# Retention pairs: a sum kept in the dead half of the raw weights, a decay table behind the values, and early output products behind the last head's values product

## The chip, the cores and the metric

The kernel runs on one core of a Trainium2 chip. Time is device time of that core in microseconds (us). A kernel is timed in several runs; one further execution is taken by the hardware profiler, and its trace is what the rows below come from. Engines are named as the profile names them: PE is the matrix engine (PEld its weight loads), DVE, ACT and POOL are the vector, scalar and GpSimd engines, SP is the engine that issues most of the loads. Line numbers such as L1198 are lines of the kernel before.

## The reference

The kernel computes a trunk of four layers on 512 tokens of 1024 channels: layer 0 and layer 3 mix tokens with a convolution module, layer 1 with neighbourhood attention, layer 2 with retention; a gated convolutional feed-forward follows each. All in float32. The change lies in the retention layer:

```python
def retention_mixer(h, w_in, log2_inv_decay, gn_g, w_out):
    q, k, v, g = jnp.split(h @ w_in, [hk, 2 * hk, 2 * hk + hv], axis=-1)
    q = rotary(q.reshape(b, s, RET_HEADS, RET_KEY_DIM)).transpose(0, 2, 1, 3)
    k = (rotary(k.reshape(b, s, RET_HEADS, RET_KEY_DIM)) * (RET_KEY_DIM ** -0.5)).transpose(0, 2, 1, 3)
    ...
    o = (o_fwd + o_bwd).transpose(0, 2, 1, 3)
    mu = jnp.mean(o, axis=-1, keepdims=True)
    var = jnp.mean(jnp.square(o - mu), axis=-1, keepdims=True)
    o = ((o - mu) * lax.rsqrt(var + EPS)).reshape(b, s, hv).astype(h.dtype) * gn_g
    return (jax.nn.silu(g) * o) @ w_out
```

`o_fwd` and `o_bwd` are sums over earlier and later tokens, weighted by a decay that falls with distance. There are 4 heads, with keys of 256 and values of 512 channels.

## The kernel before

**Precision.** A float32 operand is split into a high part (a cast on ACT, L208 for activations and L182 for weights) and a low part (a subtraction on DVE, L209 and L183). Each product is three matmuls: high by high, high by low, low by high (`mm3`, L198 to L200; for values `mm3s`, L203 to L205; the output projection has its own loop at L1420).

**Weights.** `load_w` brings a block of 128x1024 floats (512 KB) by a load that SP issues (L173) into a raw tile, tag `wr`. The pool of raw tiles has three of them (`NRAW = 3`), which all weights of the kernel take in turn: a load waits until the last reader of the tile three loads earlier is done. The halves go to pools of three as well.

**Retention.** The decay is applied as one table for each head (`table`, L1238 to L1247: a load, six instructions on DVE, an Exp on ACT; one buffer), so that a head's scores are a masked product, `scores` (L1327 multiplies by the table), and `av` multiplies scores by values, takes mean and variance of each of four banks (L1382, L1383) and normalises them (L1371). The function `gate` transposes the result (L1399), multiplies it by the gate (L1402) and splits it; `wout` multiplies by the output weights and adds into the residual in memory (`xd`); for the last two heads, `part` and `pair_wout` keep the sums of both in one bank.

**Sevens.** The projections for queries, keys and gates of heads 1 to 3 are made in pairs with seven block products in place of eight (`seven`, L1216). `sums` loads two combinations of weight blocks into a tile with tag `ws` (two of them, `RWS = 2`): a broadcast load from SP (L1172), then an accumulating load from POOL (L1175); and a fourth block d into one of two fixed tiles, `sqacc` and `dd` (L1177). `weights` (L1180 to L1201) loads a raw tile `r1`, splits it, adds its first half to the second half of the `ws` tile (L1190), splits that, adds d to that sum (L1194), and splits d and the new sum into one pair of tiles, `h4` and `l4`. The last two products of a seven need `h4` and `l4`; they are left pending and made inside the next seven or where `finish` is called; L1214 then adds the bank on DVE. Inside a seven, ACT copies sums from the bank (L1225, L1228) and writes a negated copy (L1232).

**Order.** The kernel is written once as a program; a scheduler of the language, which simulates the engines, orders each engine's instructions, with the written order as priority. `tc.issue_after(x)` holds what is written in it behind instruction x. Each engine then runs its own list in order. The loop over heads stands at L1453: table, scores, gate products, `av`, the next head's queries and keys, gate, values, output.

Of the kernel before, what the change touches and what calls it, by code (L numbers as in the profile page):

```python
# [14 lines left out]
MUL, ADD, SUB = ALU.mult, ALU.add, ALU.subtract  # L15
# [4 lines left out]
D = 1024  # L20
# [78 lines left out]
def tile_trunk(  # L99
# [7 lines left out]
    nc = tc.nc  # L107
# [9 lines left out]
    def nm(s):  # L117
        uid[0] += 1
        return f"{s}{uid[0]}"
# [9 lines left out]
    psa, psb = "a", "b"  # L129

    def bank(which):
        return cur[which].tile([P, T], F32, tag="ps", name=nm("ps"))
# [43 lines left out]
    def load_w(src, n, eng=nc.vector):  # L176
        return split_w(load_raw(src, n), n, eng)
# [19 lines left out]
    def mm3(o, wh, wl, ah, al, first, last, free=False):  # L197
        nc.tensor.matmul(o, wh, ah, start=first, stop=False, skip_group_check=free)  # L198
        nc.tensor.matmul(o, wh, al, start=False, stop=False, skip_group_check=free)  # L199
        nc.tensor.matmul(o, wl, ah, start=False, stop=last, skip_group_check=free)  # L200

    def mm3s(o, wh, wl, ah, al, first, last):
        nc.tensor.matmul(o, ah, wh, start=first, stop=False)  # L203
# [3 lines left out]
    def split(src, hi, lo, n=None):  # L207
        state["cast"] = nc.scalar.copy(hi, src)  # L208
        return nc.vector.tensor_tensor(lo, src, hi.bitcast(F32), SUB)  # L209
# [38 lines left out]
    state = {"late": [], "squares": []}  # L248
# [881 lines left out]
    def ret(after):  # L1130
        LR = 2
        with ExitStack() as st:
# [47 lines left out]
            def weights(src, r13, d):  # L1180
                n = T
                if MACC:
                    r1 = load_raw(src[:, :D], D)
                    w1 = acc_w(r1, src[:, :D], D)
                else:
                    r1 = load_raw(src[:, :D], D)
                    w1 = split_w(r1, D, nc.vector)
                w13 = split_w(r13, D, nc.vector)
                r2 = r13[:, n:]
                nc.vector.tensor_tensor(r2, r2, r1[:, :n], ADD)  # L1190
                h2 = rp.tile([P, T], F32R, tag="h2", name=nm("h2"))
                l2 = rp.tile([P, T], F32R, tag="l2", name=nm("l2"))
                split(r2, h2, l2)
                nc.vector.tensor_tensor(r13[:, :n], r2, d, ADD)  # L1194
                h4 = rp.tile([P, D], F32R, tag="h4", name=nm("h4"))
                l4 = rp.tile([P, D], F32R, tag="l4", name=nm("l4"))
                split(d, h4[:, n:], l4[:, n:])
                split(r13[:, :n], h4[:, :n], l4[:, :n])  # L1198
                u = lambda w, b: (w[0][:, b * n:(b + 1) * n], w[1][:, b * n:(b + 1) * n])
                return {"a11": u(w1, 0), "a22": u(w1, 1), "s3": u(w13, 0), "s1": u(w13, 1),  # L1200
                        "s2": u((h2, l2), 0), "sg": u((h4, l4), 0), "a12": u((h4, l4), 1)}  # L1201
# [36 lines left out]
            def table(h):  # L1238
                tb = rp.tile([P, DTAB], F32, tag="dt", name=nm("dt"))
                nc.scalar.dma_start(tb, rel)  # L1240
                for c in (slice(0, DTAB // 2), slice(DTAB // 2, DTAB)):
                    t2 = t512()[:, :DTAB // 2]
                    nc.vector.tensor_scalar(t2, tb[:, c], 0.0, lgam[:, 4 + h:5 + h], ALU.min, MUL)
                    nc.vector.tensor_scalar(tb[:, c], tb[:, c], 0.0, lgam[:, h:h + 1], ALU.max, MUL)
                    nc.vector.tensor_tensor(tb[:, c], tb[:, c], t2, SUB)
                nc.scalar.activation(tb, tb, AF.Exp)
                return tb  # L1247
# [36 lines left out]
            def vproj(h):  # L1284
                pss = [bank(psb if h == 0 else psa) for _ in range(4)]
                for kc in range(4):
                    if h in VACC:
                        wh, wl = load_w_acc(ret_v[h, kc], D)
                        for t in range(3):
                            for tb in range(4):  # L1290
                                for i in range(2):
                                    k = kc * 2 + i
                                    q = slice(tb * P, (tb + 1) * P)
                                    nc.tensor.matmul(
                                        pss[tb], (xhi, xlo)[t == 1][k][:, q],
                                        (wh, wl)[t == 2][:, i * T:(i + 1) * T],
                                        start=k == 0 and t == 0, stop=k == KD - 1 and t == 2)
                        continue
                    wh, wl = load_w(ret_v[h, kc], D)
                    for tb in range(4):  # L1300
                        for i in range(2):
                            k = kc * 2 + i
                            s = slice(i * T, (i + 1) * T)
                            q = slice(tb * P, (tb + 1) * P)
                            mm3s(pss[tb], wh[:, s], wl[:, s], xhi[k][:, q], xlo[k][:, q],
                                 k == 0, k == KD - 1)
                vv = []
                for tb in range(4):
                    hi = rp.tile([P, T], F32R, tag=f"v{tb}h", name=nm("vh"))
                    lo = rp.tile([P, T], F32R, tag=f"v{tb}l", name=nm("vl"))  # L1310
                    t = t512()
                    nc.scalar.activation(t, pss[tb], AF.Copy, scale=rstd_col[:, tb:tb + 1])
                    split(t, hi, lo)
                    vv.append((hi, lo))
                return vv
# [94 lines left out]
            def wout(h, yy, outs=range(4)):  # L1410
                for o2 in outs:
                    acc = h in WACC
                    w = load_w_acc(ret_out[h, o2], D) if acc else load_w(ret_out[h, o2], D)
                    pss = [bank(psa), bank(psa)]
                    for t in ((0, 1), (2,)) if acc else ((0, 1, 2),):
                        for oi in range(2):
                            for e in range(4):
                                s = slice((oi * 4 + e) * P, (oi * 4 + e + 1) * P)
                                for j in t:
                                    nc.tensor.matmul(pss[oi], w[j == 2][:, s], yy[e][j == 1],  # L1420
                                                     start=e == 0 and j == 0, stop=e == 3 and j == 2)
                    for oi in range(2):
                        r = t512()
                        nc.scalar.copy(r, pss[oi])
                        nc.gpsimd.dma_start(xd[o2 * 2 + oi], r, accum_op=ADD)
# [23 lines left out]
            vv = vproj(0)  # L1449
            for p in range(4):  # L1450
                combos(p)
            gs = None
            for h in range(RH):  # L1453
                tb = table(h)
                aa = scores(h, qk, tb)
                if h < 3:
                    gs, rest = g_seven(h) if h or G0 else gproj(h)
                else:
                    finish()
                    rest()  # L1460
                    wout(2, yy, (3,))
                oo = av(h, aa, vv)
                if h < 3:
                    qa, qb = seven("q", h + 1, 0), seven("q", h + 1, 1)
                    rest()
                    qk = rope(0, qa)
                    yy = gate(h, oo, gs, 0, 4)
                    finish()
                    qk += rope(1, qb)
                    vv = vproj(h + 1)  # L1470
                    if h < 2:
                        wout(h, yy)
                    else:
                        gs, rest = g_seven(3)
                else:
                    wout(2, yy, (2,))
                    for k in range(KD):
                        x[k] = const.tile([P, T], F32, tag=f"x{k}", name=nm("x"))
                        nc.gpsimd.dma_start(x[k], xd[k])
                    early = [[bank(psa), bank(psa)] for _ in range(2)]  # L1480
                    pair_wout(early[0], 2, 0, yy, True, False)
                    w = load_w(ret_out[2, 1], D)
                    part(early[1][0], w, yy, 0, True, False)
                    y3 = gate(h, oo, gs, 0, 4)
                    part(early[1][1], w, yy, 1, True, False)
                    for o2 in (0, 1):
                        pair_wout(early[o2], 3, o2, y3, False, True)
                    for o2 in (2, 3):
                        pair_wout([bank(psa), bank(psa)], 3, o2, y3, True, True)
# [215 lines left out]
```

## Time and profile before

| | us |
|---|---|
| median of 3 runs | 2529.01 |
| lowest and highest run | 2528.30, 2531.76 |
| the profiled execution | 2530.51 |
| its span | 2528.6 |
| PE busy in it | 2502.4 |
| DVE, ACT, POOL busy | 1862.7, 1319.8, 409.0 |

Mean granted clock of PE over the span is 0.997 of full speed. The retention layer lies between about 1180 and 1600 us of the span.

A row of the timeline is: start in us, duration in us, engine, line, operation, output<-inputs by the program's names, sizes, how many instructions the row joins (x3), and in brackets how long the engine stood idle before it and what ended that. A row of waits is: engine, what waited, what ended the wait, then total us, how many times, longest. The ends of matmuls are modelled, so the spacing of their starts is the better measure.

### The profile page before, as it was taken

The page shows a single profiled execution, that of the slowest core. Times are in us where ns is not written, and L with a number is a line of the kernel's source. Part 1 is how long each engine was busy: PE and PEld are TensorE (multiplying, and loading weights), DVE is VectorE, ACT ScalarE, POOL GpSimd, SP SyncE. Part 2 cuts the span into 40 slices and gives each one's busy share as a digit, 9 for nine tenths or more (in the row PEclk, how much of TensorE's full clock was granted, in tenths as well). Part 3 has the DMA queues.
Part 4 walks back from the last instruction along what each step waited for, and adds up shares of the span by engine and source line. Part 5 has one row for each costly group of instructions (what it writes and reads, how often), then busy time and mean ns, then how long its engine had stood idle before and what let it go on. Part 6 is the DMA issues. An engine that isn't in the chain of part 4 may idle for free.

```text
span 2528.6 us, 39896 instructions
## 1 busy us (share of the span) xinstructions
PE 2502.4 (99%) x15598; PEld 2186.9 (86%) x15598; DVE 1862.7 (74%) x2993; ACT 1319.8 (52%) x1888; POOL 409.0 (16%) x483
## 2 busy tenths in 40 slices
PE   9999999999999999999999999999999999999999
PEld 7888898989998889898889888779898888789897
DVE  7976867677777786767767576786767887686765
ACT  5454645465656565545444444464545445464543
POOL 2214010103320201120121211201010121201010
PEclk9999999999999999999999999999999999999999
DMA  7736676746553567776355544467674673477664
GB/s 255 228 97 185 189 163 175 166 142 163 141 134 108 141 166 168 190 177 187 87 120 149 133 113 117 131 180 164 175 167 142 201 226 91 125 191 164 175 163 133
DMA packets 140253, 399.54 MB, mean 158 GB/s; under 512 B 16368, under 2 KB 23408, under 8 KB 140064
## 3 DMA queue, kind: packets, MB, share of 16 engines
q1 hardware_dynamic: 95232, 285.69, 35.0%
q0 software_dynamic: 43248, 107.59, 23.3%
q10 hardware_dynamic: 1584, 3.70, 0.4%
q8 instruction: 122, 2.00, 0.3%
q14 instruction: 67, 0.55, 0.1%
HBM read 355.02 MB, written 38.13 MB: 155 GB/s over the span
## 4 chain that ended last, share of the span: by engine, by line
PE 88%; issue 4%; DVE 3%; DMA 3%; ACT 1%; POOL 0%; SPq 0%; DVEq 0%; POOLq 0%; ACTq 0%
PE ps L198 21%; PE ps L199 21%; PE ps L200 21%; PE ps L203 3%; PE ps L204 3%; PE ps L205 3%; PE ps L333 3%; PE ps L328 3%; PE ps L329 3%; PE ps L1420 2%; DMA wl<-in_f_up 2%; PE ps L791 1%; PE ps L789 1%; PE ps L790 1%; DMA ws<-in_ret_us 1%
## 5 line engine op out<-in xcount | busy, mean ns | idle before, releaser
L182 ACT CAST wh<-wr 128x1024 fp32r<-128x1024 f32 (+1 forms) x299 | 305.8, 1027 | 382.5 <-PE ps L199 264.7
L183 DVE TENSOR_TENSOR wl<-wr,wh 128x1024 fp32r<-128x1024 f32 (+1 forms) x296 | 359.4, 1216 | 134.5 <-ACT wh L182 123.3
L200 PE MATMUL ps<-xh,wl 128*128 128x512 f32 (+1 forms) x1112 | 427.9, 385 | 0.1
L198 PE MATMUL ps<-xh,wh 128*128 128x512 f32 (+1 forms) x1112 | 426.9, 385 | 0.5 <-ACT wh L182 0.5
L199 PE MATMUL ps<-xl,wh 128*128 128x512 f32 (+1 forms) x1112 | 427.2, 384 | 0.0
L198 PEld LDWEIGHTS ps<-xh,wh 128*128 128x128 f32 x1112 | 209.0, 188 | 45.5 <-ACT wh L182 1.3
L199 PEld LDWEIGHTS ps<-xl,wh 128*128 128x128 f32 x1112 | 209.2, 188 | 44.4 <-DVE xl L270 0.5
L200 PEld LDWEIGHTS ps<-xh,wl 128*128 128x128 f32 x1112 | 209.0, 188 | 44.3 <-DVE wl L183 0.5
L199 PE MATMUL ps<-Hl,wh 128*128 128x256 f32 (+1 forms) x734 | 224.2, 307 | 0.0
L198 PE MATMUL ps<-Hh,wh 128*128 128x256 f32 (+1 forms) x734 | 221.7, 308 | 0.0
L200 PE MATMUL ps<-Hh,wl 128*128 128x256 f32 (+1 forms) x734 | 221.3, 307 | 0.0
L328 PE MATMUL ps<-xh,wh 128*128 128x512 f32 x408 | 161.6, 396 | 0.0
L329 PE MATMUL ps<-xl,wh 128*128 128x512 f32 x408 | 161.1, 395 | 0.0
L204 PE MATMUL ps<-wl,xh 128*128 128x256 f32 (+1 forms) x512 | 159.2, 312 | 0.0
L205 PE MATMUL ps<-wh,xl 128*128 128x256 f32 (+1 forms) x512 | 158.8, 311 | 0.0
L203 PE MATMUL ps<-wh,xh 128*128 128x256 f32 (+1 forms) x512 | 157.5, 313 | 0.9 <-ACT xh L267 0.8
L198 PEld LDWEIGHTS ps<-Hh,wh 128*128 128x128 f32 x734 | 138.4, 189 | 11.5 <-ACT wh L182 4.3
L199 PEld LDWEIGHTS ps<-Hl,wh 128*128 128x128 f32 x734 | 138.2, 188 | 7.3
L200 PEld LDWEIGHTS ps<-Hh,wl 128*128 128x128 f32 x734 | 137.1, 188 | 7.3
L194 POOL DMA_DIRECT2D wl<-in_f_up x51 | 44.5, 873 | 461.0 <-ACT wl L193 366.1
L198 PE MATMUL ps<-Hh,h 128*128 128x256 f32 x384 | 108.5, 283 | 0.0
L199 PE MATMUL ps<-Hl,h 128*128 128x256 f32 x384 | 108.5, 283 | 0.0
(366 smaller groups left out, 6733.9 us busy)
## 6 DMA issues: line engine op xcount, KB each, us to landing
wr<-in_f_up SPq DMA_DIRECT2D x144, 512.0 KB, 4.0
wraw<-in_cdw SPq DMA_DIRECT2D x56, 608.0 KB, 5.3
wl<-in_f_up POOLq DMA_DIRECT2D x51, 512.0 KB, 7.9
xd<-t POOLq DMA_DIRECT2D x84, 256.0 KB, 6.1
wr<-in_f_down SPq DMA_DIRECT2D x32, 512.0 KB, 6.1
ws<-in_f_down SPq DMA_DIRECT2D x32, 512.0 KB, 7.8
ws<-in_f_down POOLq DMA_DIRECT2D x32, 512.0 KB, 8.4
wr<-in_cw_in SPq DMA_DIRECT2D x30, 512.0 KB, 4.3
```

Source lines behind the costliest of these rows:

```text
L182: nc.scalar.copy(hi[:, :n], raw[:, :n])
L183: eng.tensor_tensor(lo[:, :n], raw[:, :n], hi[:, :n].bitcast(F32), SUB)
L198: nc.tensor.matmul(o, wh, ah, start=first, stop=False, skip_group_check=free)
L199: nc.tensor.matmul(o, wh, al, start=False, stop=False, skip_group_check=free)
L200: nc.tensor.matmul(o, wl, ah, start=False, stop=last, skip_group_check=free)
L203: nc.tensor.matmul(o, ah, wh, start=first, stop=False)
L204: nc.tensor.matmul(o, ah, wl, start=False, stop=False)
L205: nc.tensor.matmul(o, al, wh, start=False, stop=last)
L328: nc.tensor.matmul(ps, wh[:, s], xhi[k], start=k == 0, stop=False)
L329: nc.tensor.matmul(ps, wh[:, s], xlo[k], start=False, stop=False)
L333: nc.tensor.matmul(ps, wl[:, k * P:(k + 1) * P], xhi[k], start=False, stop=k == KD - 1)
L1420: nc.tensor.matmul(pss[oi], w[j == 2][:, s], yy[e][j == 1], start=e == 0 and j == 0, stop=e == 3 and j == 2)
```

## The change

Three edits, all in the retention layer. First, the sum of r2 and d is written into the second half of `r1`, the raw weights, which nobody reads by then, and no longer into the first half of the `ws` tile. Second, the table of head 0 is made ahead of the loop over heads, and that of head h + 1 right behind `vproj(h + 1)`, so ahead of `wout(h)` and of the last `g_seven`. Third, in the last head, `mm3` records its last matmul, so that `av_end` is the last of the values product; three early blocks of output products (`early[0]` and one half of `early[1]`) are held behind it, and the reloads of `x` are written behind them.

```diff
     def mm3(o, wh, wl, ah, al, first, last, free=False):
         nc.tensor.matmul(o, wh, ah, start=first, stop=False, skip_group_check=free)
         nc.tensor.matmul(o, wh, al, start=False, stop=False, skip_group_check=free)
-        nc.tensor.matmul(o, wl, ah, start=False, stop=last, skip_group_check=free)
+        state["mm"] = nc.tensor.matmul(o, wl, ah, start=False, stop=last, skip_group_check=free)
...
                 split(r2, h2, l2)
-                nc.vector.tensor_tensor(r13[:, :n], r2, d, ADD)
+                nc.vector.tensor_tensor(r1[:, n:], r2, d, ADD)
                 h4 = rp.tile([P, D], F32R, tag="h4", name=nm("h4"))
                 l4 = rp.tile([P, D], F32R, tag="l4", name=nm("l4"))
                 split(d, h4[:, n:], l4[:, n:])
-                split(r13[:, :n], h4[:, :n], l4[:, :n])
+                split(r1[:, n:], h4[:, :n], l4[:, :n])
...
-            gs = None
+            gs, tb = None, table(0)
             for h in range(RH):
-                tb = table(h)
                 aa = scores(h, qk, tb)
...
                     vv = vproj(h + 1)
+                    tb = table(h + 1)
                     if h < 2:
                         wout(h, yy)
                     else:
                         gs, rest = g_seven(3)
                 else:
+                    av_end = state["mm"]
                     wout(2, yy, (2,))
+                    with tc.issue_after(av_end.ins):
+                        early = [[bank(psa), bank(psa)] for _ in range(2)]
+                        pair_wout(early[0], 2, 0, yy, True, False)
+                        w = load_w(ret_out[2, 1], D)
+                        part(early[1][0], w, yy, 0, True, False)
                     for k in range(KD):
                         x[k] = const.tile([P, T], F32, tag=f"x{k}", name=nm("x"))
                         nc.gpsimd.dma_start(x[k], xd[k])
-                    early = [[bank(psa), bank(psa)] for _ in range(2)]
-                    pair_wout(early[0], 2, 0, yy, True, False)
-                    w = load_w(ret_out[2, 1], D)
-                    part(early[1][0], w, yy, 0, True, False)
                     y3 = gate(h, oo, gs, 0, 4)
```

The order of PE's instructions is the same in both programs up to the first seven of head 1. The first place is SP's list from the loads of that head's weights on (`ret_us` are weights of the sevens, `ret_v` of the values, `ret_out` of the output; numbers tell buffers apart):

```order
 L173 DMA wr_13525<-in_ret_us 128x1024
 L173 DMA wr_13753<-in_ret_v 128x1024
-L173 DMA wr_13783<-in_ret_v 128x1024
 L1177 DMA sqacc<-in_ret_us 128x512
 L1172 DMA ws_13453<-in_ret_us 128x2x512
+L173 DMA wr_13783<-in_ret_v 128x1024
 L173 DMA wr_13813<-in_ret_v 128x1024
+L1172 DMA ws_13547<-in_ret_us 128x2x512
 L173 DMA wr_13843<-in_ret_v 128x1024
```

The second weight block of the values moves behind the broadcast load of a `ws` tile, and the next `ws` load moves ahead of the fourth block; the third block, `wr_13813`, takes over the tile of `wr_13525`, the `r1` of head 1's second seven.

The second place is the last seven before the last head's values product, on DVE. Before:

```order
L1190 TENSOR_TENSOR ws2440_15601<-ws2440_15601,wr2520_16045 128x512
L1194 TENSOR_TENSOR ws2440_15601<-ws2440_15601,dd1869_12708 128x512
...
L1214 TENSOR_TENSOR t2518_15979<-ps2517_15978,t2518_15979 128x512
L209 TENSOR_TENSOR l42528_16062<-dd1869_12708,h42527_16061 128x512
L209 TENSOR_TENSOR l42528_16062<-ws2440_15601,h42527_16061 128x512
```

and after:

```order
L1190 TENSOR_TENSOR ws2440_15601<-ws2440_15601,wr2523_16056 128x512
L1194 TENSOR_TENSOR wr2523_16056<-ws2440_15601,dd1869_12708 128x512
...
L1214 TENSOR_TENSOR t2521_15990<-ps2520_15989,t2521_15990 128x512
L209 TENSOR_TENSOR l42531_16073<-dd1869_12708,h42530_16072 128x512
L209 TENSOR_TENSOR l42531_16073<-wr2523_16056,h42530_16072 128x512
```

The last reader of the raw tile `wr` was the add at L1190, and is now the split behind the finish add at L1214; that of the `ws` tile was this split. On ACT, in the same place of the changed program, the cast of the block that takes this raw tile over (`wr2609`) stands ahead of the seven's negated copy (L1232):

```order
L208 CAST h42530_16072<-dd1869_12708 128x512
L208 CAST h42530_16072<-wr2523_16056 128x512
L182 CAST wh2610_16461<-wr2609_16459 128x1024
L1232 ACTIVATE t2535_16081<-ps2532_16078 128x512
```

As before, ACT splits, casts and only then copies.

The third place is PE's list where the last head's values product ends (`vh`, `ah`; bank `ps2585`). Before:

```order
L198 MATMUL ps2585_16376<-vh2504_15949,ah2556_16231 128x512
L199 MATMUL ps2585_16376<-vl2505_15950,ah2556_16231 128x512
L200 MATMUL ps2585_16376<-vh2504_15949,al2557_16232 128x512
L198 MATMUL ps2614_16472<-yh2461_15738,wh2618_16477 128x512
L199 MATMUL ps2614_16472<-yl2462_15739,wh2618_16477 128x512
```

and after:

```order
L198 MATMUL ps2585_16376<-vh2504_15949,ah2556_16231 128x512
L199 MATMUL ps2585_16376<-vl2505_15950,ah2556_16231 128x512
L200 MATMUL ps2585_16376<-vh2504_15949,al2557_16232 128x512
L1420 MATMUL ps2602_16424<-yh2457_15727,wh2599_16419 128x512
L1420 MATMUL ps2602_16424<-yl2458_15728,wh2599_16419 128x512
```

Before, the rest of the second early block follows (`ps2614`); after, the second half of the output products of `wout(2, yy, (2,))` (`ps2602`, 12 matmuls) and then four early blocks of 12. The four banks of the values product now advance together and end one close behind the other; before, they ended one after another.

## The prediction

> **What bounds the kernel now.** I read the page's first part first, then PE's waits over the retention layer (1180 to 1640 us of the span), then busy time and granted clock around each wait.
>
> ```profile
> span 2528.6 us, 39896 instructions
> PE 2502.4 (99%) x15598; PEld 2186.9 (86%) x15598; DVE 1862.7 (74%) x2993; ACT 1319.8 (52%) x1888; POOL 409.0 (16%) x483
> ```
>
> PE (TensorE) is busy for 99% of the span, and the change removes none of its products. What can move is the 1% in which PE stands, and what a stand does to its clock. Four waits of the retention layer are long enough for the view of waits to name them:
>
> ```profile
> PE ps L198 <- ACT t L1228: 4.0, 1, 4.0
> PE ps L199 <- DVE yl L209: 1.9, 1, 1.9
> PE ps L198 <- ACT yh L208: 0.8, 1, 0.8
> PE ps L1420 <- DVE t L1214: 0.8, 1, 0.8
> ```
>
> Behind the two longest PE works at about half clock. In the next view the columns are the window, its length, busy time and count for PE, PEld, DVE, ACT and POOL, then the granted clock, the DMA share and GB/s:
>
> ```profile
> 132.00:136.00 4.00, 2.44 (x19) 2.48 (x20) 3.76 (x6) 1.60 (x3) 0.83 (x2) 0.70 0.11 25
> ...
> 1478.00:1482.00 4.00, 0.26 (x1) 0.27 (x2) 0.56 (x1) 1.63 (x3) 0.00 (x0) 0.98 0.33 66
> 1482.00:1486.00 4.00, 4.00 (x23) 4.00 (x23) 3.58 (x6) 2.31 (x5) 0.00 (x0) 0.59 0.17 57
> 1584.00:1588.00 4.00, 3.03 (x7) 2.46 (x8) 2.72 (x5) 0.62 (x1) 0.00 (x0) 0.53 0.45 131
> 1588.00:1592.00 4.00, 4.00 (x12) 3.09 (x12) 0.00 (x0) 0.00 (x0) 0.00 (x0) 0.61 0.00 0
> ```
>
> After the 4.0-us wait, 4 us at a clock of 0.59 lose (1 - 0.59) x 4 = 1.6 us; with the 0.98 of the window before I take 1.7. After the pair 0.8 and 1.9, two windows at 0.53 and 0.61 lose 1.9 + 1.6 = 3.4 us, twice as much. So a wait has two prices: itself, and 1.7 us or twice that when the clock drops. It drops already for a shorter wait outside this layer:
>
> ```profile
> 133.56 0.85 PE L766 MATMUL ps<-ident,t 128*128 128x128 f32 x3 [1.93 <-DVE t L760]
> ```
>
> 1.93 us of idle, and the window 132 to 136 has clock 0.70. I use as an estimate: a wait of 1.9 us or more costs 1.7 us on top, one under 1 us nothing. The Trainium skill, TensorE: Matmul & The Clock Gate, section "Part 1: The HAM clock gate (the "warmup" mystery)", has the clock fall after a whole idle window of about 3.4 us; by that rule no new wait under 3.4 us would cost clock, and the sum below would come out 1 to 3 us lower. The row of 133.56 with its window of 0.70 contradicts it, and I go by the row.
>
> **What the first edit removes.** The 4.0-us wait, from its cause to its end:
>
> ```profile
> 1451.06 0.68 DVE L209 TENSOR_TENSOR l<-ws,h 128x512 fp32r<-128x512 f32 x1
> ...
> 1468.67 0.68 DVE L209 TENSOR_TENSOR l<-ws,h 128x512 fp32r<-128x512 f32 x1
> ...
> 1469.38 0.38 SPq L1172 DMA_DIRECT2D ws<-in_ret_us  x1
> ...
> 1474.48 0.87 POOL L1175 DMA_DIRECT2D ws<-in_ret_us  x1 [29.60 <-DMA ws<-in_ret_us]
> ...
> 1480.37 1.04 ACT L182 CAST wh<-ws 128x1024 fp32r<-128x1024 f32 x1 [6.68 <-DMA ws<-in_ret_us]
> ...
> 1481.74 0.50 PE L198 MATMUL ps<-ch,wh 128*128 128x256 f32 x1 [4.00 <-ACT t L1228]
> ```
>
> The last reader of a `ws` tile is the split of the sum (the L209 at 1468.67, end 1469.35), and the next load of that tile leaves SP right then. Broadcast load, accumulating load and landing take until 1480.37, 11.0 us. ACT waits there, and its copy at L1228, which PE wants, stands behind it. With the sum in `r1`, the tile's last reader is the split of r2, at 1451.06, end 1451.74. The same 11.0 us then end at 1462.7, against a need at about 1477.7 (1481.74 - 4.00): 15 us of margin. **Gain 4.0 + 1.7 = 5.7.**
>
> **What the third edit removes.** The tail of the last head:
>
> ```profile
> 1571.22 0.40 PE L200 MATMUL ps<-vh,al 128*128 128x512 f32 x1
> 1571.46 0.39 PE L198 MATMUL ps<-yh,wh 128*128 128x512 f32 x1
> ...
> 1577.51 1.53 DVE L1371 TENSOR_SCALAR o<-ps,sm,sm 128x512 f32<-128x512 f32 x2
> 1580.46 2.07 DVE L1402 SCALAR_TENSOR_TENSOR t<-ps,par,g 128x512 f32<-128x512 f32 x3 [1.42 <-PE ps L1399]
> ...
> 1581.91 1.20 PE L198 MATMUL ps<-yh,wh 128*128 128x512 f32 x4 [0.84 <-ACT yh L208]
> 1584.97 0.79 PE L199 MATMUL ps<-yl,wh 128*128 128x512 f32 x1 [1.86 <-DVE yl L209]
> ```
>
> From the last values product (1571.22) normalisation, transposes, gate and splits need 13.7 us until the first split lets PE go on at 1584.97; PE has 33 products and 16 transposes to cover them. In the new order 60 products stand there (the last 12 of `wout(2, yy, (2,))` and 48 early ones): 27 more at 0.23 us (1571.22 to 1571.46 is 0.24) are 6.3 us of cover against 0.84 + 1.86 = 2.7 us of waits. But all four values banks now end within the last 3 us, so DVE normalises four banks in one piece and not two and two; today the last scaling ends at 1577.51 + 1.53, 7.4 us behind the products' end at 1571.6, and the first pair's two scalings of another 1.53 now fall behind the products too: 9 us. The 48 products ahead of most transposes last 11 us, so these aren't late, and the first split of the gate comes about when it is wanted. I leave 0.4 us of waits. **Gain 2.7 + 3.4 - 0.4 = 5.7.** The 0.8 at L1420, a wait for a bank read at L1214, also goes, since that product now stands behind the values: **0.8**. All gains: 12.2 us.
>
> **What the first edit adds.** The raw-weight tile `r1` is one of three in a ring shared with all other weights. Its last reader was the add at L1190; it becomes the split of the sum, which DVE has behind the finish add (L1214) and the split of d:
>
> ```profile
> 1269.54 0.68 DVE L1190 TENSOR_TENSOR ws<-ws,wr 128x512 f32<-128x512 f32 x1
> 1270.25 2.60 SPq L173 DMA_DIRECT2D wr<-in_ret_v  x2
> 1282.54 0.69 DVE L209 TENSOR_TENSOR l<-ws,h 128x512 fp32r<-128x512 f32 x1
> 1282.69 1.05 ACT L182 CAST wh<-wr 128x1024 fp32r<-128x1024 f32 x1 [0.28 <-ACT h L208]
> 1286.08 0.87 PE L203 MATMUL ps<-wh,xh 128*128 128x512 f32 x3
> ...
> DMA to landing us min/median/max: 3.4/4.0/6.5
> ```
>
> Today the third weight block of `vproj(1)` leaves at 1270.25, as L1190 ends. It will leave at 1282.54 + 0.69 = 1283.3, 13 us later. Behind it on SP stand the next weights; behind its cast on ACT the negated copy at L1232. Landing is 3.4 to 6.5, median 4.0 (the last line, raw-weight loads from 1260 to 1580). With 4.0 and a cast of 1.05 the weights are there at 1288.4 to 1288.5, and PE wants them at 1286.08: **loss 2.4**, and as 2.4 lies above the 1.93 that dropped the clock but may fall astride two of its windows, 1.2 of the 1.7: 3.6 in all. The Trainium skill, DMA: Bandwidth & Descriptors, section "Anatomy of one DMA — SWDGE (gpsimd) path", fits a transfer issued by GpSimd as 2.0 us and its bytes at 436 KB per us, 3.2 us for 512 KB; by that estimate the loss here would be 1.6 us and each one below 0.8 us smaller. The rows never go under 3.4, so I keep 4.0.
>
> The same at the second head:
>
> ```profile
> 1383.54 0.69 DVE L209 TENSOR_TENSOR l<-ws,h 128x512 fp32r<-128x512 f32 x1
> ...
> 1389.71 0.40 PE L203 MATMUL ps<-wh,xh 128*128 128x512 f32 x1
> ```
>
> The load leaves at 1384.3, lands at 1388.3; then the cast (1.05, L1232 starts 0.95 after it) and L1232 (0.59) free the bank that the product of 1389.71 writes: 1389.9. **Loss 0.2**, from nothing at a landing of 3.4 to 2.7 at 6.5. At the third head the order leaves the same chain a little more room; I put nothing, with 2.2 as the upper end (the same 2.5 us of later landing).
>
> The last head has it worst:
>
> ```profile
> 1527.24 0.33 SPq L173 DMA_DIRECT2D wr<-in_ret_out  x1
> ...
> 1542.28 0.69 DVE L1214 TENSOR_TENSOR t<-ps,t 128x512 f32<-128x512 f32 x1 [7.77 <-PE ps L200]
> 1543.49 0.68 DVE L209 TENSOR_TENSOR l<-ws,h 128x512 fp32r<-128x512 f32 x1
> ...
> 1543.64 1.05 ACT L182 CAST wh<-wr 128x1024 fp32r<-128x1024 f32 x1 [0.29 <-ACT h L208]
> 1544.59 0.59 ACT L1232 ACTIVATE t<-ps 128x512 f32<-128x512 f32 x1
> ...
> 1541.96 0.28 PE L200 MATMUL ps<-xh,l 128*128 128x256 f32 x1
> 1542.08 0.28 PE L198 MATMUL ps<-ch,wh 128*128 128x256 f32 x1
> ```
>
> The third output block leaves today at 1527.24 and will leave at 1543.49 + 0.68 + 0.1 = 1544.3, land at 1548.3; cast and L1232 end 0.95 + 0.59 later, with 0.1 for the hand-over: 1549.9. PE, from 1542.08 on, has 12 products of 256 columns (0.12 each, 1541.96 to 1542.08) and 12 of 512 (0.23 each) before it writes the bank that L1232 reads: until 1546.3. **Loss 3.6 + 1.7 of clock = 5.3** (3.0 + 1.7 at the fastest landing, 6.1 + 1.7 at the slowest). The x reloads, moved behind the early pairs in the code, keep their wait for the residual sums; for them, and for the broadcast loads that now stand ahead of weights on SP, I put 0.4.
>
> **The second edit**: the same instructions for each table (a load, six on DVE, one Exp), now written right behind the next head's values projection and no longer behind that head's output projection as well, well ahead of the scores that read them.
>
> ```profile
> 1439.35 0.45 DVE L1244 TENSOR_SCALAR dt<-dt,lg 128x448 f32<-128x448 f32 x1
> ```
>
> No wait of PE named above ends in the table, so it costs nothing while PE works at the output products; without that cover DVE's part would cost up to 3 us (six of about 0.5).
>
> **Sum.** Losses 3.6 + 0.2 + 5.3 + 0.4 = 9.5, gains 12.2, net gain 2.7. The profiled execution took 2530.51 (span 2528.6), so 2527.8; the median of the runs, 2529.01, lies 1.5 lower: **2526.3 us**.
>
> **Rivals.** *A, the new waits are small:* landing of 3.4 throughout and no clock drop at the first head make losses of 1.8 + 4.7 + 0.4 = 6.9, 2523.7; if the scheduler's new order absorbs them wholly, 2529.0 - 12.2 = 2516.8. For it: the load of 1270.25 lands alone on quiet queues. Against: DVE's split comes when PE finishes, and nothing in between can be moved. *B, slower:* the late raw-weight loads land in 5.5 to 6.5 us, since the tile is now refilled while broadcast and accumulating loads are under way. One microsecond of landing costs 3 us (both stalls and the second head, soon the third), so the gain is gone at a landing of about 4.9, and at 6.5 the losses are (2.4 + 2.5 + 1.7) + 2.7 + 2.2 + 7.8 + 0.4 = 19.7: 2536.5. For it: the maximum of 6.5; against: the median of 4.0. *C, the tail is not recovered:* normalising four banks in one piece is longer than the 60 products; PE waits as today and the 5.7 falls away: 2532.0. Against: 6.3 us more cover. *That the first edit does nothing* would need the `ws` tile held by another reader than the sum's split; the issue at 1469.38, 0.03 us after that split's end, speaks against it.
>
> **How the numbers follow.** The forecast (losses between 7 and 12 us) 0.47; A 0.30; B 0.14; C 0.09. Two runs of this kernel that differ by under 0.2%, 5.1 us, can't be told apart, so faster means under 2523.95 and slower over 2534.1. A lies there but for its slow edge, and so does the fast edge of the forecast: faster 0.28 + 0.10 = 0.38. Slower is B's far half and a little of C: 0.09. The rest is 0.53. The range: A's middle, between 2516.8 and 2523.7, is 2519 at the lower end; B's near half, 2533, at the upper. The forecast's own range is 2524 to 2529.
>
> **What would show it.** Right: no wait of PE at L198 for ACT L1228 near 1478 and the `ws` load issued some 18 us earlier; new waits of 2 to 3 us in `vproj(1)` for the cast of the third block, and of 3 to 4 us ahead of the last head's values products, with clock below 0.8 behind the latter; at most 0.5 us of waits at the gate of the last head. Wrong: raw-weight loads that still leave as L1190 ends, or a wait for DVE's yl at the tail like today's.

## The result and the profile after

| | before | after |
|---|---|---|
| median of the runs (us) | 2528.91 | 2513.90 |
| lowest and highest | 2525.89, 2531.76 | 2513.04, 2518.33 |
| the profiled execution, its span | 2530.51, 2528.6 | 2517.64, 2515.9 |
| ratio, 95% interval | | 0.9945 [0.9932, 0.9958] |

The change is 14 us faster (10.6 to 17.2 by the interval; the medians lie 15.0 apart). The prediction said 2526.3 in a range of 2519 to 2533, with no change as the likeliest class. It was wrong, and the time lies below the range.

The first part of the page and PE's waits in the retention layer, after:

```profile
span 2515.9 us, 39892 instructions
...
PE 2496.7 (99%) x15598; PEld 2183.1 (87%) x15598; DVE 1865.9 (74%) x2993; ACT 1321.4 (53%) x1888; POOL 409.7 (16%) x483
```

```profile
PE ps L199 <- DVE yl L209: 0.4, 1, 0.4
```

Of the four waits of before (4.0, 1.9, 0.8 and 0.8 us) one of 0.4 is left. Busy time and clock by windows, after, over the places of the old stalls (window, its length, PE, PEld, DVE, ACT, POOL, granted clock, DMA share, GB/s):

```profile
1470.00:1490.00 20.00, 20.00 (x157) 19.36 (x157) 14.23 (x23) 8.49 (x14) 1.68 (x2) 1.00 0.61 164
1570.00:1590.00 20.00, 19.56 (x91) 15.65 (x90) 13.82 (x18) 10.51 (x17) 3.86 (x2) 1.00 0.39 136
```

PE has no gap near 1478 and full clock at both places. The two profiled executions differ by 12.7 us of span: 7.5 - 0.4 = 7.1 us of waits and, by the clock rows of before, 1.7 + 3.4 = 5.1 us of half clock; 0.5 us lies elsewhere. So the 12.2 us that the prediction summed up as gains are there, and the 9.5 us that it summed up as losses are not. The medians are further apart than the profiles, since the profiled execution of the changed kernel lies 3.7 us above that kernel's median and that of the kernel before 1.6 us above its own; the last section has a reason for such spread.

### The profile page after: what moved, and what is told of

It is laid out like the page before. It is cut to its first block, busy times and chain, and to the rows that moved or that the text cites. A ratio compares the mean times of both kernels' runs of the same rounds, so it can differ in the third digit from the quotient of the medians.

```text
span 2515.9 us, 39892 instructions
## 1 busy us (share of the span) xinstructions
PE 2496.7 (99%) x15598; PEld 2183.1 (87%) x15598; DVE 1865.9 (74%) x2993; ACT 1321.4 (53%) x1888; POOL 409.7 (16%) x483
## 4 chain that ended last, share of the span: by engine, by line
PE 89%; issue 5%; DMA 3%; DVE 2%; ACT 1%; POOL 1%; SPq 0%; DVEq 0%; POOLq 0%; ACTq 0%
PE ps L198 21%; PE ps L200 21%; PE ps L199 21%; PE ps L204 3%; PE ps L203 3%; PE ps L205 3%; PE ps L333 3%; PE ps L328 3%; PE ps L329 2%; PE ps L1420 2%; DMA wl<-in_f_up 2%; PE ps L791 1%; PE ps L790 1%; PE ps L789 1%; PE ps L1030 1%
## 5 line engine op out<-in xcount | busy, mean ns | idle before, releaser
L198 PEld LDWEIGHTS ps<-Hh,wh 128*128 128x128 f32 x734 | 138.4, 189 | 11.4 <-ACT wh L182 4.3
```

## The experiments

Each ran in five or more timed runs beside runs of the kernel before on the same chip. Times are medians. The ratio to before, with its interval, isn't quite the quotient of the two medians. Some expectations name kernels by short labels, which stand in the table.

| kernel | us | before | ratio, 95% interval |
|---|---|---|---|
| whole change, again | 2516.69 | 2528.10 | 0.9951 [0.9938, 0.9963] |
| first edit | 2519.45 | 2527.72 | 0.9968 [0.9956, 0.9981] |
| second edit (`e2_table`) | 2518.09 | 2527.72 | 0.9965 [0.9952, 0.9979] |
| third edit (`e3_early`) | 2528.38 | 2527.72 | 1.0004 [0.9995, 1.0013] |
| first and third | 2521.31 | 2527.72 | 0.9974 [0.9964, 0.9984] |
| first and second | 2514.29 | 2528.10 | 0.9945 [0.9933, 0.9958] |
| second and third | 2517.48 | 2528.10 | 0.9960 [0.9946, 0.9973] |
| third, products behind the transposes | 2523.36 | 2528.10 | 0.9978 [0.9969, 0.9988] |
| before, tiles in fixed turn (`s_before`) | 2527.16 | 2527.70 | 0.9997 [0.9988, 1.0006] |
| whole change, tiles in fixed turn (`s_after`) | 2515.57 | 2527.70 | 0.9946 [0.9933, 0.9960] |
| last head's table alone | 2522.71 | 2526.85 | 0.9977 [0.9968, 0.9987] |
| whole change, products behind the transposes | 2514.31 | 2526.85 | 0.9948 [0.9936, 0.9961] |

### The first edit alone

```diff
-                nc.vector.tensor_tensor(r13[:, :n], r2, d, ADD)
+                nc.vector.tensor_tensor(r1[:, n:], r2, d, ADD)
...
-                split(r13[:, :n], h4[:, :n], l4[:, :n])
+                split(r1[:, n:], h4[:, :n], l4[:, :n])
```

> The first edit alone (the sum in the raw tile's dead half), the table and the early blocks as before. PE's order is that of before but for some 50 products, and the tail of the last head keeps its 33 products behind the values. Theory A (the raw tile held longer costs nothing, because a load takes whichever of the three raw tiles is read out first and not the next one in turn): the wait of 4.0 us at L198 and its half clock are gone, 5.7 us faster, no new wait of PE; the waits of 1.9 and 0.8 at the tail stay. Theory B (as predicted: a ring of three in fixed turn, so the late release costs 9.5): 3.8 us slower, with new waits of 2 to 4 us in the values projection of head 1 and ahead of the last head's values product.

Measured: 8.3 us faster (5 to 11 by the interval, so 5.7 is inside, and 3.8 slower is out). PE's waits of this kernel:

```profile
PE ps L198 <- ACT yh L208: 2.2, 1, 2.2
PE ps L198 <- ACT t L1228: 0.9, 1, 0.9
PE ps L1420 <- DVE t L1214: 0.8, 1, 0.8
```

The 4.0-us wait is gone, and in the way that was predicted. The `ws` load (the first of two in its row) leaves as the split of r2 ends, and ACT finds the weights there when it comes to cast them; the split of the sum, now out of the raw tile, comes 17 us behind that load:

```profile
1447.82 0.69 DVE L209 TENSOR_TENSOR l<-ws,h 128x512 fp32r<-128x512 f32 x1
1448.53 11.54 SPq L1172 DMA_DIRECT2D ws<-in_ret_us  x2
...
1465.43 0.68 DVE L209 TENSOR_TENSOR l<-wr,h 128x512 fp32r<-128x512 f32 x1
1465.47 1.05 ACT L182 CAST wh<-ws 128x1024 fp32r<-128x1024 f32 x1 [0.86 <-PE ps L199]
```

The 0.9 us is no rest of it but a new wait, one seven later, with no half clock behind. It is a loss of the kind that theory B priced, and theory A's "no new wait" misses it:

```profile
1476.06 0.68 DVE L209 TENSOR_TENSOR l<-wr,h 128x512 fp32r<-128x512 f32 x1
1476.77 10.26 SPq L173 DMA_DIRECT2D wr<-in_ret_v  x3
...
1484.37 1.05 ACT L182 CAST wh<-wr 128x1024 fp32r<-128x1024 f32 x1 [6.40 <-DMA wr<-in_ret_v]
```

A raw weight load leaves 0.03 us behind the split of the sum (1476.06 + 0.68), takes 7.5 us to land, and PE waits for the copy at L1228, which stands on ACT behind this load's cast. It costs 0.9 us at one place, the last head's values, and not 9.5 at several. The tail waits 2.2 in place of 2.7.

### The second edit alone

```diff
-            gs = None
+            gs, tb = None, table(0)
             for h in range(RH):
-                tb = table(h)
...
                     vv = vproj(h + 1)
+                    tb = table(h + 1)
```

> The second edit alone (the table behind the values projection). As predicted: no change, within 1 us; waits of 4.0, 1.9 and 0.8 us stay. Rival, from the order: with the table written earlier the scheduler puts the last head's scores and values product ahead of the early output blocks, 60 products behind the values as in the whole change, so that this edit alone takes the tail's 2.7 us of waits and 3.4 us of half clock, about 6 us faster, with the 4.0-us wait left.

Measured: 9.6 us faster (5 to 12), for an edit priced at nothing. The rival was right, and said too little: the 4.0-us wait is gone too. PE's waits of this kernel:

```profile
PE ps L1399 <- DVE o L1371: 0.8, 2, 0.4
PE ps L199 <- DVE yl L209: 0.4, 1, 0.4
PE ps L198 <- ACT qkh L208: 0.3, 1, 0.3
PE ps L198 <- DVE t L1214: 0.2, 1, 0.2
```

The mechanism stands on DVE's timeline ahead of the scores of the head before the last (L1327 multiplies them by the table). Before:

```profile
1436.85 0.81 DVE L1243 TENSOR_SCALAR t<-dt,lg 128x448 f32<-128x448 f32 x2
...
1439.71 1.15 DVE L1245 TENSOR_TENSOR dt<-dt,t 128x448 f32<-128x448 f32 x2
1441.65 1.23 DVE L183 TENSOR_TENSOR wl<-ws,wh 128x1024 fp32r<-128x1024 f32 x1 [0.79 <-ACT wh L182]
1443.91 2.48 DVE L1327 SCALAR_TENSOR_TENSOR t<-ps,dt 128x512 f32<-128x512 f32 x4 [1.04 <-ACT dt L1246]
```

and with the whole change:

```profile
1435.21 0.68 DVE L209 TENSOR_TENSOR l<-wr,h 128x512 fp32r<-128x512 f32 x1
1435.82 2.48 DVE L1327 SCALAR_TENSOR_TENSOR t<-ps,dt 128x512 f32<-128x512 f32 x4
```

Before, DVE makes the table right ahead of the scores (with two weight splits between), and their multiplication by the table waits for its Exp on ACT. Made earlier, the table lets it start at 1435.8 in place of 1443.9, 7 us earlier after the 1 us by which the two traces are apart there. The head's values, the sevens' splits and the `ws` loads follow: in the kernel with this edit alone the load of the stalled `ws` tile leaves 8 us earlier, though the sum still stands in that tile:

```profile
1460.33 0.69 DVE L209 TENSOR_TENSOR l<-ws,h 128x512 fp32r<-128x512 f32 x1
...
1461.05 0.38 SPq L1172 DMA_DIRECT2D ws<-in_ret_us  x1
```

Before, these two stood at 1468.67 and 1469.38, behind the four scalings of the head's result. The edit moves the table and, through the scheduler, the order of what follows; the runs don't separate the two.

### The third edit alone

```diff
                 else:
+                    av_end = state["mm"]
                     wout(2, yy, (2,))
+                    with tc.issue_after(av_end.ins):
+                        early = [[bank(psa), bank(psa)] for _ in range(2)]
+                        pair_wout(early[0], 2, 0, yy, True, False)
...
```

> The third edit alone (early output blocks behind the last head's values product). 51 products stand behind the values, 18 more than before, 4.2 us of cover against 2.7 us of waits. As predicted for this edit: the waits at the tail go, 6.5 us faster (2.7 + 3.4 + 0.8 - 0.4), the 4.0-us wait stays. Rival: the early blocks are behind the values but the table is late, so the values product itself is late or PE waits at the scores; gain under 3 us.

Measured: no change. Neither side of the expectation describes it: PE doesn't wait elsewhere, it waits as before. PE's timeline at the tail of this kernel:

```profile
1567.42 0.40 PE L200 MATMUL ps<-vh,al 128*128 128x512 f32 x1
...
1576.06 0.60 PE L1399 MATMUL ps<-ident,o 128*128 128x128 f32 x4
...
1579.30 1.47 PE L1399 MATMUL ps<-ident,o 128*128 128x128 f32 x12
1581.61 1.20 PE L198 MATMUL ps<-yh,wh 128*128 128x512 f32 x4 [0.84 <-ACT yh L208]
1584.67 0.56 PE L199 MATMUL ps<-yl,wh 128*128 128x512 f32 x1 [1.86 <-DVE yl L209]
```

The values end 4 us earlier than before (1567.4 and 1571.2), with 48 products behind them and not 33 (the expectation's 51 counts three too many). But all 48 stand ahead of the last twelve transposes, and the gate's chain, which starts at those transposes, has nothing beside it. The same 0.84 and 1.86 us come out.

### The third edit, with the last early block behind the transposes

```diff
-                        nc.tensor.transpose(ps[:, ib * P:(ib + 1) * P],
-                                            oo[ib][:, e * P:(e + 1) * P], ident)
+                        state["tr"] = nc.tensor.transpose(ps[:, ib * P:(ib + 1) * P],
+                                                          oo[ib][:, e * P:(e + 1) * P], ident)
...
                     y3 = gate(h, oo, gs, 0, 4)
-                    part(early[1][1], w, yy, 1, True, False)
+                    with tc.issue_after(state["tr"].ins):
+                        part(early[1][1], w, yy, 1, True, False)
```

> The third edit alone, and the last early block (12 products) held behind the last transpose of the gate. Products behind the values: 51, as in e3_early, which kept both tail waits; products behind the transposes: 12 in place of none. Theory E (the tail waits because nothing stands between the last transpose and the products that need the gate, whatever stands behind the values): the waits of 0.8 and 1.9 fall below 0.8 together and the half clock behind them mostly goes, 3 to 5 us faster than e3_early and than before. Theory of the prediction (what counts is how much stands behind the values): no change against e3_early, waits of 2.7 us.

Measured: 4.7 us faster than before (3 to 8). Its waits:

```profile
PE ps L198 <- ACT t L1228: 3.8, 1, 3.8
PE ps L1420 <- DVE t L1214: 0.8, 1, 0.8
PE ps L203 <- DVE t L1214: 0.8, 1, 0.8
PE ps L198 <- ACT qkh L208: 0.2, 1, 0.2
PE ps L198 <- DVE t L1214: 0.2, 1, 0.2
```

Both waits of the gate are gone, with the same 48 products behind the values; 12 of them now stand behind the last transpose. Over all kernels the last wait goes by that count: none behind the last transpose in before, the first, the third and the first and third edit (2.2 to 2.7 us of waits), 5 in the kernels with the whole second edit (0.4), and 9 or 12 in this one and the two at the end of the experiments (none).

### The edits in pairs

First and third:

> First and third edit, the table as before. If the table edit does nothing and the others add up: 12 us faster, as much as the whole change but for what can't be told apart (its median is 15.0 us faster). If the table edit is needed for the order of the tail: 6 to 9 us faster, with a wait of over 1 us at the last head's gate or its scores.

First and second:

> First and second edit, the early output blocks as before (third edit left out). Theory C (the third edit does nothing by itself once the table is early, since e2_table already had the early blocks behind the values): the whole gain, 13 to 15 us. Theory D (all three are needed): 3 us or more short of the whole change, with a wait of over 1 us at the last head's gate.

Second and third:

> Second and third edit, the sum in the ws tile as before (first edit left out). Theory C: as the second edit alone, 9 to 10 us, with the waits of 0.4 and 0.4 at the transposes near 1478 that it left. If the first edit is worth 5.7 beside the others: 9 us. If the first edit's gain is taken already by the table, which moved the split of the sum forward on DVE: 13 us or more.

The whole change beside them on the same chip as the last two:

> The whole change once more, on the same chip as the next three. All theories: 13 to 15 us faster than before; no wait of PE in the retention layer over 0.5 us.

The whole change came out 11.4 us faster on this chip (9 to 16 by the interval), by its median less than the 13 to 15 that all theories had; its one wait of PE in the retention layer is 0.4 us, as in the first profile of it. First and third are 6.4 us faster, not told apart from the first alone; the tail waits 2.7 us as before, so the table is what orders the tail. There is a wait of 1.1 us at L1228 too, of the same kind as the 0.9 of the first edit: its load leaves at 1477.87, 0.03 us behind the split of the sum. First and second have the whole gain (13.8 us faster): theory C, the third edit adds nothing that can be measured. Second and third are 10.6 us faster; the interval overlaps that of the whole change, so what the first edit adds beside the second isn't settled by time. By its profile it is 1 us of waits, two of 0.4 at the transposes near 1476 and one of 0.2 at 1478. The first and second edit each alone take the 4.0-us wait, by different ways (a tile that is free earlier, a split that runs earlier), and so their gains of 8.3 and 9.6 don't add up.

### The raw tiles in fixed turn

```diff
-        raw = wraw.tile([P, D], F32, tag="wr", name=nm("wr"))
+        raw = wraw.tile([P, D], F32, tag=f"wr{turn[0] % NRAW}", name=nm("wr"), bufs=1)
+        turn[0] += 1
```

> The kernel before, with the three raw weight tiles given out in fixed turn (three names of one buffer each) for the whole kernel. A control for s_after. If tiles were taken in turn anyway: the same time as before. If each load takes the tile that is free first (theory A): the same or some us slower, where turns and release order differ today.

> The whole change, with the three raw tiles given out in fixed turn. Theory A (the change escaped the late release because a load takes the tile that is free first): here the predicted losses come back. The third block of the values waits for the split of the sum at each head, and so does an output block at the last head: waits of PE of 2 to 4 us in at least two places, 5 to 10 us slower than the whole change, close to or above s_before less 5. Rival (the late release costs nothing for another reason, for instance because the blocks have time enough): within 2 us of the whole change.

In the changed kernel the third block of `vproj(1)` didn't wait for the split of the sum. DVE and SP, after:

```profile
1270.57 1.23 DVE L183 TENSOR_TENSOR wl<-wr,wh 128x1024 fp32r<-128x1024 f32 x1 [0.31 <-ACT wh L182]
...
1281.84 0.68 DVE L209 TENSOR_TENSOR l<-wr,h 128x512 fp32r<-128x512 f32 x1
...
1271.82 0.33 SPq L173 DMA_DIRECT2D wr<-in_ret_v  x1
...
1282.70 0.33 SPq L173 DMA_DIRECT2D wr<-in_ret_out  x1
```

It left at 1271.82, as another raw tile came free (the weight split of 1270.57 ends at 1271.80). The tile that holds the sum went to a block of the output weights, at 1282.70, right behind the split's end (1282.52). So the section on the kernel before is wrong in that the raw tiles are taken in turn, and the section on the change in that the third block takes over the tile of `wr_13525`. That is theory A's reading, and the two kernels in fixed turn test whether it is what saved the time. It isn't: the changed kernel in fixed turn is as fast as the changed kernel (ratio 0.9946, control 0.9997). There a values block did leave late, right behind the split of the sum (lines are 3 higher):

```profile
1281.33 0.69 DVE L212 TENSOR_TENSOR l<-wr,h 128x512 fp32r<-128x512 f32 x1
...
1282.18 0.33 SPq L176 DMA_DIRECT2D wr<-in_ret_v  x1
```

```profile
PE ps L202 <- DVE yl L212: 0.4, 1, 0.4
```

and PE waits for nothing but the old 0.4 at the tail. The rival holds. The reason, read from the order and not tested by itself: the scheduler knows the late release, and its order for PE has the finish products (24 of 256 columns) ahead of that block's products and not behind them. With the table late, in the first edit alone and in first and third, PE had nothing else to do at one place, and the late release cost 0.9 and 1.1 us.

### The last head's table alone

```diff
-                tb = table(h)
+                if h < 3:
+                    tb = table(h)
                 aa = scores(h, qk, tb)
...
                     vv = vproj(h + 1)
+                    if h == 2:
+                        tb = table(3)
```

> Of the second edit only the last head's table: table(3) behind vproj(3), the other three at the head of the loop as before; first and third edit left out. PE's order is that of before up to the last head, and there 60 products stand behind the values, 9 of them behind the gate's last transpose. Theory F (the table stands right ahead of the scores on DVE, so where it is late it delays scores, values and all that follows in that head): the tail's waits of 0.8, 1.9 and 0.8 go with the half clock behind them, the 4.0-us wait at 1478 and its half clock stay; 5 to 6 us faster, between before and the whole second edit (9.6 faster). Rival (the tail's gain in e2_table came down from the earlier heads): the tail waits as before, no change.

Measured: 4.1 us faster (3 to 8; the 5 to 6 expected lie inside). Its waits:

```profile
PE ps L198 <- ACT t L1228: 4.0, 1, 4.0
PE ps L203 <- DVE t L1214: 0.7, 1, 0.7
PE ps L198 <- DVE t L1214: 0.2, 1, 0.2
```

All three waits of the tail are gone and the 4.0 stays, as theory F has it: each head's table moves the work of its own head. The rest of the second edit's 9.6 us fits the 4.0-us wait with its half clock (4.0 + 1.7 = 5.7), and so the tables of the earlier heads.

### The whole change, with the last early block behind the transposes

> The whole change, and the last early block held behind the gate's last transpose: 12 products behind the transposes in place of 5. Theory E: the last wait of the tail, 0.4 us, goes; nothing else moves; 0 to 0.5 us faster than the whole change, which can't be told from no change, 13 to 15 us faster than before. Theory of the prediction (only what stands behind the values counts): the 0.4 us stay.

Measured: 12.5 us faster than before (10 to 16), not told apart from the whole change. The view of PE's waits names none in the retention layer: the 0.4 is gone, as theory E has it. In time it makes no difference that can be measured, and neither does leaving out the third edit.

## Why the prediction was wrong

**The removed stall was right.** The 4.0-us wait goes, for the reason given: the load of the `ws` tile leaves at the earlier split. Its price, 5.7, lies in the interval of the first edit alone.

**The losses failed at one step**: "The raw-weight tile `r1` is one of three in a ring shared with all other weights", and from it "It will leave at 1282.54 + 0.69 = 1283.3". The load left at 1271.82. The row that was read as proof, the load of 1270.25 right behind L1190, shows that this load took `r1`'s tile in the kernel before; it doesn't show that the same load takes it when another tile is free first. The list of SP's loads already hinted at it: in the changed order a `ws` load and the fourth values block stand behind the third, where such a wait would hold them up as well. The losses of 3.6, 0.2 and 5.3 rest on this step and fall with it, and nothing of the 0.4 for the reloads was seen. The fixed-turn kernel, where a values block did leave late, shows that they would have fallen anyway. The mechanism itself exists: with the table late, a load did wait for the split of the sum, and PE for it, 0.9 us in the first edit alone and 1.1 in first and third. That was in the projection of the last head's values, where the prediction put nothing with 2.2 as the upper end, and no more of the 9.5 us was seen.

**The second edit failed at "No wait of PE named above ends in the table, so it costs nothing".** It gains 9.6 us alone. The row of 1443.91 has DVE waiting 1.04 us for the table's Exp, and the table's row at 1439.35 was quoted in the prediction; what wasn't asked is what stands behind that wait. PE was busy all the while, but with products that were then missing at the tail (33 stand behind the values there, 60 in the kernel with the second edit), and the splits behind the scores were late for the `ws` load. An engine that is always busy can still be late with the product that matters.

**The third edit failed at "PE has 33 products and 16 transposes to cover them. In the new order 60 products stand there".** The new order is right, but it comes from the second edit. Products ahead of the last transpose don't cover the chain that starts at it. The third edit alone is worth 0 where 6.5 was said, and 12 products moved behind the transposes are worth 4.7.

**The sum of the gains, 12.2, agrees with the profiles' 12.7 by luck of place**: the same waits went, but the 0.8, 1.9 and 0.8 us that were credited to the third edit went by the second.

**The rivals.** What happened is the far end of rival A, "if the scheduler's new order absorbs them wholly", 2516.8. It had no chance of its own, and the lower bound of the range, 2519, cut it off. The measured median lies another 2.9 us below it; no wait accounts for these, and how much of them is clock is open. Rival B's premise came true: in the changed kernel raw-weight loads between 1260 and 1580 take longer,

```profile
DMA to landing us min/median/max: 3.4/4.5/8.4
```

against 3.4, 4.0 and 6.5 before. Nothing on the path of PE hung on it in the whole change. Rival C, a tail that isn't recovered, is what the third edit does alone.

**The clock's price was too firm.** "A wait of 1.9 us or more costs 1.7 us on top, one under 1 us nothing" holds for the 4.0-us wait (in the five traces that have it, or 3.7 of it, half clock followed or had begun in it) but only half the time for 1.9, and the last section has half clock behind pairs of waits of 0.9. The 3.4 us for the tail are what the one profile of before has, 6.83 us at half clock; the three other traces with the same waits of 0.8 and 1.9 (third edit, first and third, before in fixed turn) have 3.41 us, which is 1.7 us of loss.

## What to carry to other kernels

Ask of an edit that moves work off a busy engine's path not whether that engine waits for it, but what else waits for it: a table that is finished just in time delays every product and split behind it, and the price shows up tens of microseconds later. Cover counts from the point where a chain starts on the engine, here the last transpose, so products must stand behind that point and not merely behind the step before. Before a buffer that is held longer is put down as a loss, two questions stand: which load takes it next in the new order, and what a scheduler can put in front of that load's users.

## What the runs showed of the hardware

A wait of 1.93 us (at L766, twice in each trace, outside the retention layer) was followed by half clock in 14 of 28 cases over 14 traces of these kernels, with the wait the same to 0.01 us. Window 132 to 136 in the kernel before had clock 0.70; in the kernel with the second and third edit, around the same wait:

```profile
132.00:136.00 4.00, 2.68 (x42) 2.71 (x43) 3.52 (x6) 1.57 (x4) 1.06 (x3) 1.00 0.15 29
```

What decides is where the wait falls. In the trace's record of the granted clock every half-clock stretch that ends inside the span is 3.41 us long or twice that, and within one trace their starts lie a whole number of 3.413 us apart (133.59 and 1481.86 in the kernel before are 395 such intervals apart). In all 14 cases the stretch began 0.0 to 1.5 us behind the wait's end. In the 12 cases without one whose trace has a stretch elsewhere to count from, the next interval would have begun 1.6 us or more behind it. So the clock fell when the whole wait lay inside one interval (3.41 - 1.93 = 1.48), and not when a bound of the intervals cut it. It need not be one wait: six more stretches stand behind two waits of 0.9 us each (L789 and L791), 0.3 us apart. In the kernel with the first and second edit:

```profile
145.93 0.28 PE L789 MATMUL ps<-W,X 128*64 128x128 f32 x1 [0.90 <-ACT W L208]
...
147.00:150.00 3.00, 2.88 (x27) 2.88 (x28) 3.00 (x6) 0.00 (x0) 0.00 (x0) 0.50 0.00 0
```

With PE's idle time summed over each interval at full clock in the 14 traces (by the modelled ends of matmuls), all 25 intervals with 1.9 us or more were followed by half clock, 7 of the 22 with 1.44 to 1.9 us, and none of the 3930 with less.

The phase differs from run to run, and at 1.7 us for each wait so struck this accounts for some of the 5 us between the lowest and the highest run of one kernel: the changed kernel's runs have mean clock 1.000 at 2513.0 to 2513.1 and 0.998 at 2518.3. How much of the rest is clock wasn't measured. The Trainium skill, TensorE: Matmul & The Clock Gate, section "Part 1: The HAM clock gate (the "warmup" mystery)", states a free-running window of 3413 ns, and the traces agree; it has the throttle come back after an idle window, and here 1.93 us of standing inside a window were enough.
